# Cutting the second- and third-last store of a streaming softmax into 16 KB rows

## The chip, the cores and the metric

The kernel runs on one core of a Trainium2 chip. The metric is the device time of one execution in microseconds (us), as the median of several runs; a run varies by about 2 us either way. The profile is of one of the timed executions; for the kernel before it is of a further one, of 2512.59 us. Its span is some 2 us under the device time of that same execution. All runs here are fast, that is undisturbed, at a granted clock of 1.0. Timed comparisons are given as a ratio with a 95% interval.

## The reference

A softmax over the last axis of logits of shape 16 x 256 x 32768 in float32, with temperature 1.0:

```python
scaled = logits / temperature
scaled = scaled - scaled.max(axis=-1, keepdims=True)
exp_scaled = np.exp(scaled)
return (exp_scaled / exp_scaled.sum(axis=-1, keepdims=True)).astype(np.float32)
```

It reads 536.87 MB and writes 536.87 MB, once each. There is almost no arithmetic per byte.

## The kernel before

Each row of 32768 is cut in half, which gives 8192 half rows of 64 KB. A **tile** is 128 of them (8.39 MB), one per partition, and there are 64 tiles, t = 0 to 63. Three buffers hold the tiles in turn, so load t + 3 waits for store t.

```python
_BUFS = 3
_LOAD = 16384
_END = 4096
...
    def load(t: int) -> None:
        n = _END if t in (0, G - 1) else _LOAD
        for s in range(0, W, n):
            nc.sync.dma_start(
                out=buf[t % _BUFS][:, s : s + n],
                in_=x[t * P : (t + 1) * P, s : s + n],
            )

    def store(t: int, a: int, b: int) -> None:
        nc.scalar.dma_start(
            out=o[t * P : (t + 1) * P, a:b], in_=buf[t % _BUFS][:, a:b]
        )
```

For each piece of a tile VectorE takes a maximum and ScalarE an exponential with its sum; the halves are combined; VectorE and ScalarE then scale the pieces. Every tile but the last is stored whole; the last one is stored piece by piece.

```python
            if t == G - 1:
                store(t, a, c)
        if t < G - 1:
            store(t, 0, W)

    with tc.manual_schedule():
        for t in range(_BUFS):
            load(t)
        for t in range(G):
            normalise(t)
            if t + _BUFS < G:
                load(t + _BUFS)
```

A transfer of a whole tile has rows of 64 KB ("bulk" below). One of a piece of 4096 columns has rows of 16 KB ("fine"). Loads are issued by SyncE and use queue q1; stores are issued by ScalarE and use queue q10.

## Time and profile before

| | before |
|---|---|
| median of the first 3 runs | 2516.56 us |
| span of the profiled run | 2510.7 us |
| VectorE busy, ScalarE busy | 63%, 54% |
| DMA moved, mean | 1073.91 MB, 428 GB/s |
| VectorE's longest wait near the end | 16.5 us, for load 63 |

In all lines DVE is VectorE, ACT ScalarE, POOL GpSimd and SP SyncE; a q behind the name means the engine's sequencer, which issues transfers. The names are those of the program: x is the tile, nm its negated maxima, f the factors that scale it. In the slices of the page each digit is the busy share of one fortieth of the span, in tenths. The chain of waits gives a start in us, a length, and what it was. A line of the queue view gives packets, MB, and the share of the time of 16 DMA engines. The prediction below shows these lines for the kernel before. Beside these views I used the trace's packet records: one record for each row that a DMA engine moved, and a 4-byte one for each engine's completion of a transfer, sixteen to a transfer; a transfer has landed at the last of them. The records don't name the engine, but linked end to start they fall into sixteen chains.

### The profile page before, as it was taken

How to read it: one execution, taken by the hardware profiler on the slowest of the kernel's cores; microseconds unless marked ns; L12 is line 12 of the kernel's file. 1: busy time of each engine (PE TensorE's matmuls, PEld its weight loads, DVE VectorE, ACT ScalarE, POOL GpSimd, SP SyncE). 2: the span in 40 equal slices, each digit the busy share in tenths (PEclk: the TensorE clock that was granted, in tenths of full speed). 3: DMA queues.
4: the chain of work that ended last, by engine and by line, in shares of the span. 5: the costliest groups of instructions: out<-in, count | busy, mean ns of one | idle time of the engine just before them, and what ended most of it. 6: DMA issues, size and time to landing. Idle time of an engine off the chain costs nothing.

```text
span 2510.7 us, 2617 instructions
## 1 busy us (share of the span) xinstructions
DVE 1575.7 (63%) x1216; ACT 1368.1 (54%) x895; POOL 0.2 (0%) x4
## 2 busy tenths in 40 slices
DVE  6465766657656666576665665766656657666573
ACT  6445646546455465564554645645546456465463
POOL 0000000000000000000000000000000000000000
DMA  9999999999999999999999999999999999999996
GB/s 401 389 427 434 433 433 434 434 433 434 435 433 434 434 432 423 434 434 432 434 434 433 434 433 433 434 434 434 433 434 434 434 433 434 432 427 434 434 427 296
DMA packets 19748, 1073.91 MB, mean 428 GB/s; under 512 B 2192, under 2 KB 2192, under 8 KB 2192
## 3 DMA queue, kind: packets, MB, share of 16 engines
q1 hardware_dynamic: 10080, 536.88, 49.7%
q10 hardware_dynamic: 9648, 536.88, 49.6%
q14 instruction: 20, 0.16, 0.0%
HBM read 536.87 MB, written 536.87 MB: 428 GB/s over the span
## 4 chain that ended last, share of the span: by engine, by line
DMA 72%; DVE 17%; ACT 9%; another core or an unknown queue 2%; issue 0%; SPq 0%; ACTq 0%
DMA x<-in_logits_dram 36%; DMA out_dram<-x 35%; DVE nm L99 12%; ACT x L106 7%; DVE x L135 4%; ACT x L139 2%; DVE f L131 0%; ACT ee L116 0%; DVE rS L130 0%; DVE Sh L78 0%; DVE ttj L119 0%; DVE Sh L75 0%; SPq L62 0%; ACTq L68 0%
## 5 line engine op out<-in xcount | busy, mean ns | idle before, releaser
L99 DVE TENSOR_REDUCE nm<-x 128x1 f32<-128x4096 f32 x318 | 1117.6, 3579 | 701.6 <-DMA x<-in_logits_dram 701.6
L106 ACT ACTIVATE x<-x,nm 128x4096 f32<-128x4096 f32 x318 | 965.4, 3036 | 1043.5 <-DVE nm L99 1043.5
L139 ACT ACTIVATE x<-x,f 128x2048 f32<-128x2048 f32 (+1 forms) x194 | 371.2, 1975 | 75.1 <-DVE f L131 73.7
L135 DVE TENSOR_SCALAR x<-x,f 128x4096 f32<-128x4096 f32 (+2 forms) x194 | 372.2, 1975 | 2.5 <-DVE f L131 0.2
L119 DVE CUSTOM_DVE_ANT_0 ttj<-ee,ssum 128x5 f32<-128x5 f32 (+1 forms) x64 | 10.6, 166 | 196.7 <-ACT ee L116 196.7
L106 ACT ACTIVATION_READ_ACCUMULATOR x<-x,nm 128x1 f32 x318 | 59.3, 186 | 0.0
L116 ACT ACTIVATE ee<-nm,nMh 128x5 f32<-128x5 f32 (+1 forms) x64 | 18.2, 284 | 0.0
L131 DVE TENSOR_SCALAR f<-ee,rS 128x5 f32<-128x5 f32 (+1 forms) x64 | 14.8, 231 | 2.2
L130 DVE RECIPROCAL rS<-Sh 128x1 f32<-128x1 f32 x64 | 10.5, 164 | 2.2
L78 DVE TENSOR_TENSOR nMh<-nMh 128x1 f32<-128x1 f32 x64 | 10.2, 159 | 2.2
L78 DVE TENSOR_TENSOR Sh<-Sh 128x1 f32<-128x1 f32 x64 | 10.2, 159 | 2.2
L114 DVE TENSOR_REDUCE nMh<-nm 128x1 f32<-128x5 f32 (+1 forms) x64 | 10.1, 157 | 2.2
L75 DVE STREAM_SHUFFLE Sh<-Sh 128x1 f32<-128x1 f32 x64 | 9.7, 151 | 0.0
L75 DVE STREAM_SHUFFLE nMh<-nMh 128x1 f32<-128x1 f32 x64 | 9.7, 151 | 0.0
L106 ACT ACT_TABLE_LOAD x1 | 1.3, 1283 | 8.1 <-DMA x<-in_logits_dram 8.1
L119 DVE DVE_READ_ACCUMULATOR2_ANT Sh<- 128x1 f32 x64 | 5.2, 82 | 0.0
L75 DVE LOAD_MASK_SELECT nMh<-nMh x64 | 0.9, 14 | 2.8
L75 DVE LOAD_MASK_SELECT Sh<-Sh x64 | 0.9, 14 | 2.8
L170 POOL MEMSET const-bfloat16-1.0<- 128x1 bf16 x1 | 0.1, 102 | 0.0
L170 POOL MEMSET const-uint8-127<- 128x1 uint8 x1 | 0.1, 102 | 0.0
L170 POOL MEMSET const-float32-0.0<- 128x1 f32 x1 | 0.1, 99 | 0.2 <-issue 0.2
L170 POOL MEMSET const-float32-1.0<- 128x1 f32 x1 | 0.1, 99 | 0.0
## 6 DMA issues: line engine op xcount, KB each, us to landing
x<-in_logits_dram SPq DMA_DIRECT2D x8, 2048.0 KB, 23.7
out_dram<-x ACTq DMA_DIRECT2D x4, 2048.0 KB, 10.7
out_dram<-x ACTq DMA_DIRECT2D x63, 44.3
x<-in_logits_dram SPq DMA_DIRECT2D x62, 43.6
```

Of the source, the lines that this page charges most:

```text
L75: nc.vector.stream_shuffle(out=v[:, j + 1 : j + 2], in_=v[:, j : j + 1], mask=mask)
L78: nc.vector.tensor_tensor(out=v[:, j + 1 : j + 2], in0=v[:, j : j + 1], in1=v[:, j + 1 : j + 2], op=op,)
L99: nc.vector.tensor_reduce(out=nm[:, k : k + 1], in_=xc, axis=X, op=A.max, negate=True)
L106: nc.scalar.activation(out=xc, in_=xc, func=Exp, bias=nm[:, k : k + 1], scale=inv_t, accum_out=ssum[:, k : k + 1],)
L114: nc.vector.tensor_reduce(out=nMh[:, 0:1], in_=nm, axis=X, op=A.min)
L116: nc.scalar.activation(out=ee, in_=nm, func=Exp, bias=nMh[:, n_rounds : n_rounds + 1], scale=-1.0)
L119: nc.vector.tensor_tensor_reduce(out=ttj, in0=ee, in1=ssum, scale=1.0, scalar=0.0, op0=A.mult, op1=A.add, accum_out=Sh[:, 0:1],)
L130: nc.vector.reciprocal(out=rS, in_=Sh[:, n_rounds : n_rounds + 1])
L131: nc.vector.tensor_scalar_mul(out=f, in0=ee, scalar1=rS)
L135: nc.vector.tensor_scalar_mul(out=xs[:, a:b], in0=xs[:, a:b], scalar1=f[:, k : k + 1])
L139: nc.scalar.activation(out=xs[:, b:c], in_=xs[:, b:c], func=Copy, scale=f[:, k : k + 1])
L170: nc = _bacc.Bacc("TRN2", target_bir_lowering=False, num_devices=1)
```

## The change

Its intent: near the end, the last load should not have to share the DMA engines with stores of larger packets. Stores 61, 62 and 63 are issued as transfers of 16 KB rows. Store 63 and load 63 were fine already.

```diff
+_FINE_STORES = 3
...
     def store(t: int, a: int, b: int) -> None:
-        nc.scalar.dma_start(
-            out=o[t * P : (t + 1) * P, a:b], in_=buf[t % _BUFS][:, a:b]
-        )
+        n = _END if t >= G - _FINE_STORES else b - a
+        for s in range(a, b, n):
+            nc.scalar.dma_start(
+                out=o[t * P : (t + 1) * P, s : s + n],
+                in_=buf[t % _BUFS][:, s : s + n],
+            )
```

## The prediction

> **What bounds the kernel now.** I read the page first: busy shares, slices, queues, chain. A name used below: tile t is one block of 128 half rows (8.39 MB), t from 0 to 63; three buffers hold them in turn, so load t+3 can only be issued when store t has landed.
>
> ```profile
> DVE 1575.7 (63%) x1216; ACT 1368.1 (54%) x895; POOL 0.2 (0%) x4
> ...
> DMA  9999999999999999999999999999999999999996
> GB/s 401 389 427 434 433 433 434 434 433 434 435 433 434 434 432 423 434 434 432 434 434 433 434 433 433 434 434 434 433 434 434 434 433 434 432 427 434 434 427 296
> DMA packets 19748, 1073.91 MB, mean 428 GB/s; under 512 B 2192, under 2 KB 2192, under 8 KB 2192
> ...
> DMA 72%; DVE 17%; ACT 9%; another core or an unknown queue 2%; issue 0%; SPq 0%; ACTq 0%
> ```
>
> No compute engine passes 63%. The DMA engines are full in every slice but the last, at about 434 GB/s; only the last slice (62.8 us long, 296 GB/s) has room. About 20 us of DMA time are lost there (62.8 x (1 - 296/434)). Nothing before that slice can gain from the change, since loads and stores share one full resource. So next I cut the end into windows:
>
> ```profile
> 2420.00:2432.00 12.00, 12.00 (x3) 7.05 (x3) 0.00 (x0) 1.00 1.01 437
> 2440.00:2448.00 8.00, 6.75 (x11) 6.82 (x6) 0.00 (x0) 1.00 1.01 432
> 2456.00:2466.00 10.00, 4.92 (x2) 7.70 (x6) 0.00 (x0) 1.00 1.02 441
> 2472.00:2488.00 16.00, 6.62 (x13) 4.97 (x4) 0.00 (x0) 1.00 0.01 6
> 2491.00:2508.00 17.00, 2.08 (x2) 3.15 (x2) 0.00 (x0) 1.00 0.98 417
> ```
>
> The last two columns are the DMA share and GB/s. The loss is one hole, 2472 to about 2489 us. The chain of waits says what fills it:
>
> ```profile
> 2442.12 5.81 DVE x L135 x3
> 2447.94 12.98 DVE nm L99 x3
> 2460.92 16.49 another core or an unknown queue
> 2477.41 0.02 issue
> 2477.43 4.43 DVE nm L99
> 2481.86 0.02 issue
> 2481.89 3.80 ACT x L106 x2
> ```
>
> VectorE has the maxima of three pieces of tile 63 by 2460.9 and then waits 16.5 us. The chain calls it an unknown queue, but the view of waits gives it to the load: its line for VectorE is 27.0 us in two waits for the logits, longest 16.5. The fourth piece was issued at 2417.3 and landed 60.1 us later. Why so late, when the DMA is at full rate? The queue view of two stretches:
>
> ```profile
> q10 hardware_dynamic: 64, 4.19, 80.8%
> q1 hardware_dynamic: 64, 1.05, 20.4%
> ```
>
> This is 2421 to 2433 us: stores (q10) and loads (q1) had 64 packets each, but the stores moved 4.19 MB and the loads 1.05 MB. Turns are shared one packet each, and a packet of store 61 is a whole 64 KB row, one of load 63 is 16 KB. The load that the end waits for gets a fifth.
>
> ```profile
> q10 hardware_dynamic: 51, 3.34, 85.6%
> q1 hardware_dynamic: 9, 0.15, 3.8%
> ```
>
> This is 2457 to 2466 us: the same again against store 62, now only on the few engines that are still behind with load 63. The packet records show the 16 completion packets of piece four from 2451.4 to 2477.1 us: thirteen engines are through by 2457, one at 2466, one at 2469, and one at 2477. That **late engine** has been 6 to 7 us behind since the start of the program (completions of nearly every bulk transfer spread by 7.1 us).
>
> **What the Trainium skill says.** "DMA: Bandwidth & Descriptors", section "Queues, rings and completion order": each DMA engine goes round the queues that have work and switches only at packet boundaries. The trace agrees (64 to 64 packets, bytes four to one). The page has packets of some 9 to 17 descriptors; here the records count 128 packets of 65,536 B in a bulk store and 128 of 16,384 B in a fine one, so one row is one turn, and this measurement decides. The same page, "Why a DMA increments its semaphore by 16 and not by 1": a transfer counts as landed only when all participating engines have posted. Agrees: VectorE started at 2477.4, after the sixteenth. "Where 436 GB/s comes from": ceiling 435.2 GB/s; the trace's 430 to 437 is at it, so no change of packets can raise the rate, only fill the hole.
>
> **The change part by part.** The diff's title also speaks of queues and of the last load in 16 KB pieces and of three stores; the kernel before already has both queues, the fine last load, and the fine last store. What is new is that stores 61 and 62 go in four transfers of 16 KB rows instead of one of 64 KB rows. Compute instructions are the same. Added: 2 x 3 = 6 issues on ScalarE's sequencer at 0.34 us (the row "out_dram<-x" on its queue), 2 us. For tile 61 they fall at 2409.5, when ScalarE has nothing until about 2424; for tile 62 at about 2446, and ScalarE then waits for the next maximum until 2450.5. Both hidden: 0 us.
>
> Packet durations, medians of the records: 2.418 us for 64 KB, 0.611 us for 16 KB. Each transfer gives each engine 8 packets (128 rows over 16 engines). Follow the late engine, which ends last.
> - Before: store 60 completes at 2414.65, so load 63 is issued from 2415.2 on. Load 62 completes at 2419.5; store 61 then has 7 packets left, and 7 turns of 2.418 + 0.611 make 21.2 us (its completion: 2441.1). Then loads alone until store 62 comes at 2449. At 2451.3 piece three completes, 8 fine packets remain, each behind a 64 KB one: 8 x 3.03 = 24.2 us, with a slow packet and a turn for the completion 25.8: 2477.07.
> - After: between 2414.65 and the end of load 62 one load packet and one fine store packet pass, 3.0 us, so load 62 ends near 2417.7 instead of 2419.5. Then 31 fine store packets and 32 fine load packets take turns: 31 x 2 x 0.611 = 37.9 us, 2455.6; the last load packet and its completion behind a packet or two of store 62: **about 2457 instead of 2477**.
> - Compute: tile 62 starts 1.8 us sooner, so VectorE is free at about 2446.1; four maxima at 4.37 us, the fourth no longer waiting for long: max(2446.1 + 3 x 4.37 = 2459.2, 2457) + 4.4 = 2463.6. From the end of the last maximum to the issue of the first store took 6.9 us (2481.86 to 2488.78), to its first packet 0.84 more: 2471.4 instead of 2489.6. So 18 us sooner for the stores of tile 63.
> - But the DMA engines must be free. Thirteen finished store 62 at 2471 before and will again: their hole shrinks to about half a microsecond. The late engine was busy without a gap until 2477.07; its work is the same plus 16 split rows at 4 x 0.611 - 2.418 = 0.026 us, 0.4 us: 2477.5. Store 63 is by then queued behind it, and its four pieces took 19.83 us (2489.62 to 2509.45): 2497.3. From the last completion to the end of the span 1.2 us: 2498.5 against 2510.7.
>
> Sum: **-12.2 us**, not the 18 of the earlier landing, because the late engine becomes the bound. Taken off the median: 2516.56 - 12.2 = 2504.4. A small replay of the packet turns, with these durations, gives -12.1 with the engines in step, and the same with lateness put in.
>
> **The rivals.** (1) *Fine mixing is dearer.* Nowhere before do 16 KB loads and 16 KB stores alternate for long; the mixed stretches have a 64 KB side. Fine packets alone ran at 0.611 to 0.64 us. If alternating costs 6% more over the 40 us in which both run, 2.4 us go back: 2506.8. For it: nothing in the trace; against it: fine loads alone moved 432 GB/s, the same as bulk. (2) *The gain is hidden*: the end would be bound by something else all along. The stores of 63 would then have to be late for another reason than load 63, and the only one is VectorE's four maxima, which set 2463.6 above; the hole of 16 us has no other owner. If it were so: 2514 to 2517. (3) *Work given back*: store 61 begins slower against load 62's 64 KB packets, and the DMA has the same bytes, so store 62 and 63 might queue up further. In the count above this is included and costs the thirteen engines nothing; if the late engine fell behind by another 3 us: 2507.4. (4) *Larger gain*: the timed runs are 4 us above the profiled execution (2516.56 against 2512.59); if that is a later engine, whose penalty before the change is multiplied by five (3.03 against 0.611 us per packet), the gain is larger, up to 18 us: 2498.6.
>
> **Range and chances.** Centre 2504.4. Rivals 1 and 3 put it at 2507, a rerun adds or takes some 2 us (the three runs span 3 us), rival 4 takes up to 6 off: 2499 to 2510. The most that filling the hole can give is 20 us of 2516, 0.8%, so within 2% is all but certain: 0.98, faster by over 2% 0.01, slower 0.01.
>
> **What would show it.** In the profile after: packets under the load queue and the store queue in 2421 to 2433 near equal in bytes; the fourth piece landing about 40 us after its issue, not 60; VectorE's longest wait for it under 3 us; the DMA share of 2472 to 2488 near full; 61 bulk store issues instead of 63 and 12 fine ones instead of 4; the late engine ending some 5 us after the rest, where before all ended within 0.2 us. I am wrong if the hole stays, if packets of 16 KB grow past 0.65 us in the mix, or if the fourth piece lands before 2460 and the end still stands at 2510.

## The result

| | before | changed |
|---|---|---|
| median, 4 runs each | 2516.01 us | 2501.78 us |
| lowest to highest | 2514.04 to 2518.52 | 2501.22 to 2504.56 |
| span of the profiled run | 2510.7 us | 2499.8 us |
| packets, mean rate | 19748, 428 GB/s | 20612, 430 GB/s |

The ratio is 0.9945, interval 0.9928 to 0.9962: a real gain of about half a per cent, which counts as "same" at the threshold of 2%. A ratio is the mean time of one kernel's fast runs over the mean of the other's in the same rounds, so it is not quite the ratio of the medians.

The page of the changed kernel, its slices and its packet count:

```profile
DMA  9999999999999999999999999999999999999998
GB/s 405 398 420 435 436 434 435 435 430 434 433 433 435 435 434 435 432 434 430 433 435 436 436 427 435 431 433 428 435 433 436 426 433 436 434 429 432 433 422 373
DMA packets 20612, 1073.91 MB, mean 430 GB/s; under 512 B 2288, under 2 KB 2288, under 8 KB 2288
```

The last slice went from 296 to 373 GB/s, while the middle is as it was. The gain is at the end, as intended, but the last slice is still not full. The windows of the changed kernel, over the same stretches (length; busy time of VectorE, ScalarE and GpSimd; clock; DMA share; GB/s):

```profile
2420.00:2432.00 12.00, 12.00 (x3) 7.42 (x4) 0.00 (x0) 1.00 1.00 427
2440.00:2448.00 8.00, 7.12 (x11) 6.45 (x6) 0.00 (x0) 1.00 1.00 430
2456.00:2466.00 10.00, 9.35 (x7) 6.08 (x3) 0.00 (x0) 1.00 0.98 421
2472.00:2488.00 16.00, 6.82 (x11) 9.28 (x7) 0.00 (x0) 1.00 0.63 265
```

The hole of 2472 to 2488 is only partly filled. By the packet records most engines stop at 2471.8 and start again at 2478.7, so a hole of about 7 us remains where the prediction has half a microsecond.

The queue view of the changed kernel from 2421 to 2433 us:

```profile
q10 hardware_dynamic: 176, 2.62, 51.0%
q1 hardware_dynamic: 176, 2.62, 51.0%
```

Packet for packet as before, and now byte for byte: the load has half instead of a fifth. In each of the sixteen chains of records one row of the store and one of the load follow each other in turn but for the completions, before the change (64 KB, 16 KB, 64 KB, ...) and after it, so the equal counts come from single rows and not from batches. Load 63's last completion is at 2458.98 instead of 2477.07. From 2415 us on, the 16 KB packets of the load took 0.611 us on average and those of the stores 0.613.

So the load came 18 us sooner. The chain of waits of the changed kernel shows why its stores came only 11 us sooner:

```profile
2418.34 41.12 DMA x<-in_logits_dram
...
2459.53 0.34 ACTq L71
...
2459.92 14.87 ACT x L110 x8
...
2477.87 0.34 ACTq L71
```

Line 71 is the issue of a store on ScalarE's own sequencer. At 2459.53 it issues the fourth store of tile 62, right after the last load landed, and only then come four exponentials of tile 63 in a row. VectorE had the first maximum by 2451.9. The timeline shows the blocked sequencer (start, length, what), and the view of waits what ScalarE waited for (total, times, longest):

```profile
2446.41 13.46 ACTq L71 DMA_DIRECT2D out_dram<-x  x3
```

```profile
ACT x L110 <- DMA x<-in_logits_dram: 12.3, 1, 12.3
```

The second, third and fourth store of tile 62 stretch over 13.46 us, where three issues of 0.34 us were expected. Of ScalarE's wait of 12.3 us, some 8 come after VectorE's first maximum; the rest it would have waited anyway (4.32 us in e1 below). The built program names the cause. There are eight completion semaphores for all transfers, taken in turn, and a transfer waits until the previous user of its semaphore has landed:

```text
445 L71 DMACopy out_0_dram<-x2_60 128x4096 [waits DMAHW7_49,DVE_49]
446 L71 DMACopy out_0_dram<-x2_60 128x4096 [waits DMAHW0_49,DVE_49]
447 L71 DMACopy out_0_dram<-x2_60 128x4096 [waits DMAHW1_49,DVE_49,Activation_49]
448 L71 DMACopy out_0_dram<-x2_60 128x4096 [waits DMAHW2_49,Activation_49]
```

These are the four stores of tile 62 in the changed kernel, and semaphores 7, 0, 1 and 2 belong to the four pieces of load 63. The third store was issued at 2449.8, after piece three had landed (2449.26), and the fourth at 2459.5, after piece four (2458.98). The exponentials stand behind these issues in ScalarE's program, and the first of them started at 2459.92. The stores of tile 61 were held in the same way: the second went out at 2409.30 and the third at 2419.67, after load 62, the earlier user of its semaphore, had landed at 2419.22. That held up no exponential: the next one waited for VectorE until 2424.05.

### The profile page after: what moved, and what is told of

The parts are those of the page before. It is cut to its first block, busy times and chain, and to the rows that moved or that the text cites. A ratio compares the mean times of both kernels' runs of the same rounds, so it can differ in the third digit from the quotient of the medians.

```text
span 2499.8 us, 2623 instructions
## 1 busy us (share of the span) xinstructions
DVE 1575.8 (63%) x1216; ACT 1367.8 (55%) x895; POOL 0.2 (0%) x4
## 2 busy tenths in 40 slices
DMA packets 20612, 1073.91 MB, mean 430 GB/s; under 512 B 2288, under 2 KB 2288, under 8 KB 2288
## 4 chain that ended last, share of the span: by engine, by line
DMA 72%; DVE 14%; ACT 9%; another core or an unknown queue 4%; issue 0%; SPq 0%; ACTq 0%
DMA x<-in_logits_dram 37%; DMA out_dram<-x 36%; DVE nm L103 10%; ACT x L110 7%; DVE x L139 3%; ACT x L143 2%; DVE f L135 0%; SPq L63 0%; ACT ee L120 0%; DVE rS L134 0%; DVE Sh L82 0%; DVE ttj L123 0%; DVE Sh L79 0%; ACTq L71 0%
## 5 line engine op out<-in xcount | busy, mean ns | idle before, releaser
L134 DVE RECIPROCAL rS<-Sh 128x1 f32<-128x1 f32 x64 | 10.5, 164 | 2.2
```

The lines of the kernel that those rows point to most:

```text
L134: nc.vector.reciprocal(out=rS, in_=Sh[:, n_rounds : n_rounds + 1])
```

## The experiments

All were timed in 5 rounds against the kernel before, on one chip per group of four. Profiled runs reach the end of the loop at slightly different times. To compare ends, the table counts from the start of tile 62's first maximum in the same run, that is from the landing of load 62. In e7 load 62 lands in two halves, and the first maximum needs only the first of them; there the count is from the second maximum (2423.23 us), so its row compares less well.

| run | ratio to before, 95% interval | load 63 landed | first store of 63 issued | end of span |
|---|---|---|---|---|
| before | 1 | 57.1 | 68.8 | 90.7 |
| changed | 0.9945 (0.9928 to 0.9962) | 39.4 | 58.3 | 80.2 |
| e8, changed again | 0.9953 (0.9941 to 0.9966) | 39.8 | 58.6 | 80.4 |
| e1, two transfers | 0.9946 (0.9933 to 0.996) | 40.4 | 52.2 | 78.8 |
| e2, only store 61 fine | 0.9967 (0.9955 to 0.998) | 49.1 | 60.8 | 82.9 |
| e3, only store 62 fine | 0.9956 (0.9944 to 0.9969) | 45.6 | 57.4 | 79.5 |
| e4, bulk load, bulk stores | 0.9985 (0.9973 to 0.9998) | 38.9 | 63.5 | 85.5 |
| e5, bulk load, fine stores | 0.995 (0.9936 to 0.9963) | 25.2 | 52.1 | 78.5 |
| e6, e1 with first stores fine | 0.992 (0.9907 to 0.9932) | 41.2 | 52.9 | 78.9 |
| e7, everything fine | 0.9958 (0.9946 to 0.9971) | 39.7 | 51.5 | 78.2 |

Theory A, that of the prediction: queues take turns packet by packet, so the size of packets decides what share the last load gets; and with a fair share the end is set by the DMA engine that is furthest behind. Its main rivals: the path through VectorE, ScalarE and the first store of tile 63 sets the end; fine packets help as such.

**e1: the same packets without the semaphore wait.** Edit to the kernel before, in `store`:

```diff
-        nc.scalar.dma_start(
-            out=o[t * P : (t + 1) * P, a:b], in_=buf[t % _BUFS][:, a:b]
-        )
+        dst, src = o[t * P : (t + 1) * P, a:b], buf[t % _BUFS][:, a:b]
+        if t in (G - 3, G - 2):
+            dst = dst.rearrange("p (c h n) -> p h c n", h=2, n=_END)
+            src = src.rearrange("p (c h n) -> p h c n", h=2, n=_END)
+            for h in range(2):
+                nc.scalar.dma_start(out=dst[:, h], in_=src[:, h])
+        else:
+            nc.scalar.dma_start(out=dst, in_=src)
```

> Edit: stores 61 and 62 keep 16 KB packets but go in two transfers each instead of four, so that no store of tile 62 needs the completion semaphore of a piece of load 63 (in the changed kernel its third and fourth store wait for pieces three and four of load 63, and ScalarE's exponentials stand behind them until 2459.9 us). Theory A (the late DMA engine is the bound; the blocked ScalarE costs only what exceeds it): the exponential of the first piece starts by 2453, the first store of tile 63 is issued near 2470.5 instead of 2477.9, yet the end comes only some 2 us sooner than in the changed kernel, about 2498 us of span: 15 to 17 us under the kernel before, ratio 0.9935 to 0.994. Rival B (the path through ScalarE and the first store is the bound): the whole 7 us come through, ratio about 0.9915. Rival C (the packets are not what helped, the four transfers are): the gain of the change is lost, ratio near 1.

The packets stayed at 16 KB, and the wait is gone. The timeline of e1, and its window of the hole:

```profile
2449.49 1.49 ACTq L74 DMA_DIRECT2D out_dram<-x  x2
2453.77 3.71 ACT L112 ACTIVATE x<-x,nm 128x4096 f32<-128x4096 f32 x1 [4.32 <-DVE nm L105]
```

```profile
2472.00:2488.00 16.00, 5.94 (x4) 6.19 (x4) 0.00 (x0) 1.00 0.99 422
```

The first exponential follows VectorE's first maximum. The first store comes 52.2 us after the reference point instead of 58.3, and the hole is gone (265 to 422 GB/s). Yet the end gained only 1.4 us (80.2 to 78.8), and the timed ratio is that of the changed kernel within its interval of about 3 us either way; the 0.9935 to 0.994 expected can't be told from it. By the packet records, the last store's completions spread over 4.7 us: thirteen engines end from 2494.1 to 2494.7 us, two near 2497, and the last at 2498.9. The prediction looked for this sign in the changed kernel. There the 7 us hole had brought all engines back into step (2498.36 to 2498.54). Rival B, by which the whole of the earlier store would come through, fails (its ratio of 0.9915 lies outside the interval); so does rival C, since two transfers do as well as four.

**e2: only store 61 fine.**

```diff
-        n = _END if t >= G - _FINE_STORES else b - a
+        n = _END if t in (G - 3, G - 1) else b - a
```

> Edit: only store 61 in 16 KB packets, store 62 again one transfer of 64 KB packets. Theory A (turns per packet): load 63 meets store 61 for nearly all of its time, so it lands near 2457 us as in the changed kernel; store 62 has one semaphore to wait for, of piece one of load 63, which is early, so ScalarE isn't blocked. Gain 14 to 17 us over the kernel before, ratio 0.9935 to 0.9945, as good as the whole change. Rival (both fine stores are needed, since the 16.5 us of waiting in the kernel before fell on store 62): load 63 lands past 2465, gain under 8 us.

A miss. I had followed only the late engine, whose store 61 lasts as long as load 63. The other engines began store 61 before load 63 was issued, so they finish it early and meet the 64 KB packets of store 62 with pieces of the load still to come. Completions of the fourth piece run from 2458.2 to 2470.0 us, and VectorE waits again. The chain of waits of e2:

```profile
2461.82 8.52 another core or an unknown queue
2470.36 4.43 DVE nm L103
```

The gain is 0.33% instead of the 0.55 to 0.65% expected. The rival's numbers hold: a landing past 2465, and 7.8 us (90.7 to 82.9).

**e3: only store 62 fine.**

```diff
-        n = _END if t >= G - _FINE_STORES else b - a
+        n = _END if t >= G - 2 else b - a
```

> Edit: only store 62 in 16 KB packets, store 61 again 64 KB packets. Theory A: load 63 gets a fifth against store 61 until 2441 us, then nearly all until store 62 comes at 2448, then half: on the late engine some 15 packets are left at 2447, 15 x 1.22 = 18 us, so it lands near 2466; the first store of tile 63 near 2479 and the gain 9 to 11 us, ratio about 0.996. Rival (store 62 is what the waiting fell on, so making it fine is enough): as good as the whole change, 14 us.

The load landed at 2468.8 (expected near 2466), the first store was issued at 2480.5 (expected near 2479), and the ratio is 0.9956. Theory A's numbers hold. Each of the two stores does part of it: either one alone leaves load 63 at 45.6 or 49.1 us, and both together bring it to about 40. In time, e3's interval overlaps that of the full change, and by the profile it ends as early (79.5 us after the reference point, the changed kernel at 80.2). So the rival, that a fine store 62 is enough, isn't refuted as to time: the runs resolve no gain from a fine store 61.

**e4: no fine store at all, and a bulk last load.** Edit to the kernel before:

```diff
-        n = _END if t in (0, G - 1) else _LOAD
+        n = _END if t == 0 else _LOAD
```

> Edit to the kernel before: no fine store; instead load 63 goes as one transfer of 64 KB packets, as all other loads. Theory A (a queue's share goes by the size of its packet against the other's, not by fineness): load and store 61 have equal shares, the load lands whole near 2457 us, but VectorE can then only start on tile 63: four maxima of 4.4 us, 2475, first store issued near 2482 and the end near 2503.5 us of span: 6 to 8 us faster than before, ratio about 0.997. Rival (16 KB packets as such are what helps): the load lands no sooner than 2470, and since nothing of tile 63 is worked on before, the kernel is 5 us or more slower.

The timeline of e4, where the four maxima of tile 63 begin:

```profile
2461.66 17.40 DVE L99 TENSOR_REDUCE nm<-x 128x1 f32<-128x4096 f32 x4 [11.39 <-DMA x<-in_logits_dram]
```

With 64 KB against 64 KB the load landed 38.9 us after the reference point, as soon as with 16 KB against 16 KB (39.4). So the ratio of packet sizes decides, not their fineness. VectorE then has all four maxima still to do, so the end gains only 5.2 us by the profile and 0.15% in time, less than the 6 to 8 us expected but not the loss that the rival gave.

**e5: bulk last load against fine stores.** The edit of e4, made to e1.

> Edit to the two-transfer kernel: load 63 goes in one transfer of 64 KB packets, stores 61 and 62 stay in 16 KB packets. Theory A (share by packet size, end bound by the late DMA engine): now the load has four fifths, so it lands whole near 2445 us, 12 us or more sooner than in the changed kernel; VectorE never waits for it, first store of tile 63 near 2472; but the late engine still has the same bytes to move, so the end stays within 2 us of the two-transfer kernel, ratio about 0.9945 against before. Rival B (the landing of load 63 sets the end): 5 us or more faster than the two-transfer kernel, ratio 0.992.

Now the load has the larger packets. It landed whole after 25.2 us, 15 us sooner than in e1, and VectorE starts its maxima without waiting, straight after tile 62's scaling. The chain of waits of e5:

```profile
2440.89 5.81 DVE x L141 x3
2446.70 17.32 DVE nm L105 x4
```

The first store is issued at 52.1 us and the end is at 78.5, both as in e1. A load that lands 15 us sooner changes nothing: past a point the landing isn't what the end waits for. The store's completions again spread, from 2491.3 to 2496.0.

**e6: fine first stores too.** Edit to e1:

```diff
-        if t in (G - 3, G - 2):
+        if t in (0, 1, 2, G - 3, G - 2):
```

> Edit to the two-transfer kernel: stores 0, 1 and 2 also go in 16 KB packets. In all traces so far the stretch 45 to 90 us, where load 2 and store 0 first meet, runs at only about 350 GB/s with packets of 2.7 to 2.9 us, and the lateness of single engines (completions spread by 5 to 12 us) is there from then on. Theory A says that the lateness adds to the end one for one, so: if fine packets there cure the slow stretch, up to 8 us and some of the lateness are gained, ratio 0.990 to 0.992; if they don't, ratio as the two-transfer kernel, 0.9945, and the spread of completions still 6 to 8 us. Which, is open: no theory of the slow stretch is put forward.

Windows of the kernel before, in which load 2 meets store 0, and the stretch after it:

```profile
45.00:85.00 40.00, 21.65 (x19) 21.35 (x14) 0.00 (x0) 1.00 0.94 356
85.00:130.00 45.00, 24.61 (x19) 21.35 (x14) 0.00 (x0) 1.00 0.99 417
```

The same of e6:

```profile
45.00:85.00 40.00, 36.64 (x23) 29.36 (x19) 0.00 (x0) 1.00 0.99 426
85.00:130.00 45.00, 29.02 (x25) 26.92 (x19) 0.00 (x0) 1.00 1.03 437
```

The slow stretch is cured, and the median is 2493.16 us against 2500.61 for the changed kernel in the same rounds (e8). The intervals of the two ratios don't overlap. This is the fastest version. Worked out from the windows, 40 x (426 - 356) / 433 + 45 x (437 - 417) / 433 = 8.5 us of DMA time are recovered. In the profiled runs only 2.9 of them are left when tile 62 starts (2415.22 against 2418.11); by the packet records from 400 to 2400 us e6 moved 432.4 GB/s and the kernel before 433.2, some 4 us. At least part of that is chance: the profiled execution of e6 was its slowest, 2495.92 us against the median of 2493.16. Against e8, 7.5 of the 8.5 us arrive in the medians. The lateness was not cured: completions of early transfers are within 0.3 to 1.1 us, but by the end one engine is again some 4 to 7 us behind. So no run took the lateness away while the engines were full, and that the end would then gain these us is argued and not shown.

**e7: every load and store fine.** Edit to e1: `t < G - 1` in place of `t in (G - 3, G - 2)`, and bulk loads in two transfers of 16 KB rows in the same way.

> Edit to the two-transfer kernel: every load and store in 16 KB packets. Theory A (fineness itself costs, only the ratio at the end helps): 16 KB packets take 0.611 us, four of them 2.444 against 2.418 us for 64 KB, 1.1% more on 2450 us of full DMA: 20 to 27 us lost, so 5 to 15 us slower than the kernel before, ratio 1.002 to 1.006. Rival (fine packets as such help): ratio at or below 0.9945.

A miss: it is 0.4% faster than before instead of slower. Windows of the kernel before and then of e7, in the steady part:

```profile
400.00:2400.00 2000.00, 1273.26 (x978) 1101.89 (x721) 0.00 (x0) 1.00 1.00 433
```

```profile
400.00:2400.00 2000.00, 1264.87 (x977) 1099.57 (x721) 0.00 (x0) 1.00 1.01 431
```

By the packet records the two rates are 433.2 and 431.4 GB/s. Fine packets cost 0.4% there, under half of the 1.1% expected, in part because the bulk packets of the kernel before average 2.423 us there and not their median of 2.418; the rest the runs don't separate. That is some 8 us of these 2000. The start, which my expectation left out, runs at 432 instead of 356 GB/s from 45 to 85 us and gives 7 of them back, and the end gives about 12.5 (90.7 to 78.2, with the reservation above). It is no better than the changed kernel, so fineness everywhere isn't worth having: it pays at the two ends and costs in the middle.

**e8: the changed kernel again**, as control on the same chip.

> The changed kernel itself, as the control on the same chip and in the same rounds as the other three. Ratio 0.9945 as before; the third and fourth store of tile 62 again issued when pieces three and four of load 63 land, the first store of tile 63 about 7 us later after the landing of load 62 than in the two-transfer kernels, and the end within 2 us of theirs.

As expected: ratio 0.9953, first store 58.6 us after the reference point, against 52 to 53 in e1, e5 and e6 (6 us, where 7 were written), and the end within 2 us of theirs.

## Why the prediction was right

The measured 2501.78 us lies in the range of 2499 to 2510, 2.6 us under the centre. Of the signs named, these held: equal bytes, a landing 41.1 us after the issue (about 40 forecast), no wait of VectorE for the fourth piece, and 61 bulk and 12 fine store issues.

- **Turns per packet** was right, and is shown three ways: equal bytes at equal packets in the changed kernel, an equally early landing with bulk on both sides (e4), and a landing of 25.2 us with bulk against fine (e5). The records of single engines, one row in turn, agree. The landing itself was given as 2457 and came at 2459.0, and tile 62 started 0.4 us sooner and not 1.8: in this profiled run store 60 landed 1.5 us later (2416.18 against 2414.65), for a reason that the runs don't show. Counted from there, load 62 took 3.0 us as forecast, and load 63 took 42.8 where 42.4 were forecast.
- **Fine mixing costs nothing extra** (rival 1): 0.611 and 0.613 us per packet. That rival is out.
- **"Both hidden: 0 us" for the added issues is the step that failed.** The 0.34 us of an issue are hidden. What I left out is that an issue can wait: with eight semaphores in turn, the stores of tile 62 stood behind the pieces of load 63, and ScalarE's exponentials, behind the stores, started some 8 us later than VectorE's first maximum allowed. The first store was issued at 2477.9, not 2470.5. So the sign "half a microsecond of hole" was wrong (7 us), and so was the sign of a last engine ending 5 us after the rest.
- **The end moved by nearly what was forecast all the same**, because the late engine was nearly as late as the blocked store. It finished store 62 at 2476.98 (forecast 2477.5), and the first packets of store 63 came at about 2478.7, so the unforeseen wait cost only the difference of 1.7 us. The span went from 2510.7 to 2499.8 us, by 10.9: the forecast 12.2, less 1.7 for the wait, plus 0.5 since the late engine finished that much sooner. That the wait which the prediction didn't know of cost so little was luck. From the reference point the end moved by 90.7 - 80.2 = 10.5 us, and with the wait taken away (e1) by 11.9. That the late engine bounds these versions is shown by e1 and e5: a store issued 6 us sooner is worth 1.4 us, and a load landing 15 us sooner nothing.
- **The timed gain** was 14.2 us between medians in the first session and 12.0 in the second (e8). The profiles give 10.9. Rival 4, by which timed runs have a later engine and so a larger gain, would fit the first, but the timed runs leave no packet records. The difference of 14.2 and 10.9 lies in the kernel before: its profiled execution (2512.59) was 3.4 us under the median of that session, and near that of the second (2512.56). Whether a later engine made the first session's runs slower stays open.
- **Two readings were wrong without harm.** That only the last slice has room isn't what the lines show: the slices begin with 401, 389 and 427 GB/s, an estimated 12 us more (62.8 x (33 + 45 + 7) / 434). The change doesn't touch them, but e6 gained 7.5 us there. And "no change of packets can raise the rate" does not hold there: fine first stores raised it from 356 to 426 GB/s.

## What to carry to other kernels

Where a load that the end waits for shares the DMA engines with stores, compare the row sizes of the two: each turn moves one row, so the side with larger rows takes the larger share, and it is enough to change it where the wait is. When a transfer is cut into more transfers, look in the built program at whose semaphore each one waits for, and keep such a wait off an engine that also computes. After a wait is shortened, ask which of sixteen parallel engines is the last: the time may be that engine's own work, and sooner work elsewhere is then worth little.

## What the Trainium skill lacked or had wrong

- "DMA: Bandwidth & Descriptors", section "Queues, rings and completion order": it has turns between queues at packets of some 9 to 17 descriptors. Here one row was one packet and one turn, up to 64 KB: 64 packets each moved 4.19 MB of stores and 1.05 MB of loads in 12 us. The consequence, that a queue with larger rows takes a larger share, isn't stated.
- The same page, "Why a DMA increments its semaphore by 16 and not by 1", advises one semaphore for each transfer in flight. No page says what it costs where there are fewer: an issue that waits for an unrelated transfer, here 9.3 us for the fourth store of tile 62 (2450.2 to 2459.5) and with it ScalarE's exponentials.
- The same page, section "Latency and other measured facts", has two engines that are usually slower than the others, with a guess that ties this to transfers issued by GpSimd. No page has one that stays some 7 us behind for nearly a whole program with transfers issued by SyncE and ScalarE alone, or says what it costs at the end: the sixteen completions of store 60 spread by 7 us or more in every version with bulk stores there, and the end waited some 5 us for the last engine in e1 and e5.
- No page has the slow start of bulk against bulk: 356 GB/s from 45 to 85 us with 64 KB rows on both sides, and 426 with 16 KB stores (e6). The same mix of 64 KB rows runs at 433 later on, so row size alone is not the cause, and it stays open.
- "DMA: Bandwidth & Descriptors", section "Where 436 GB/s comes from", says that for HBM to SBUF transfers the HBM side of about 358 GB/s binds. Taken alone this is wrong here: with this one core working, reads and writes together ran at 433 GB/s over 2000 us. Elsewhere the skill keeps that figure for two cores that stream at once.
